# Linear attention in a decoder step: the norm factor of the prompt's chunks taken ahead of the decoded tokens and by tables, the gate applied to four chunks at a time

## The chip, the cores and the metric

One core of a Trainium2 chip. The metric is the time of one execution on the device, in microseconds, lower is better. Its engines here: TensorE (PE), VectorE (DVE), ScalarE (ACT), GpSimd (POOL) and SyncE (SP), whose queue issues most of the DMAs. TensorE's granted clock is 0.996 of its full 2.4 GHz in the profiled execution.

## The reference, cut to what matters

One layer of a hybrid decoder: 1024 prompt tokens and 8 sequences of 8 decoded tokens, width 1024. The part in question is the gated linear attention: 4 heads, key width 128, value width 256. Its output is normalised per token and head, multiplied by a gate, and projected:

```python
o_b, gla_state = gla_fn(q_b, k_b, v_b, log_alpha)
o_b = rmsnorm(o_b, g_gla).reshape(b, t, B_VAL_WIDTH) * jax.nn.silu(r_b)
merged = jax.nn.sigmoid(gate_a) * (o_a @ w_proj_a) + jax.nn.sigmoid(gate_b) * (o_b @ w_proj_b)
# rmsnorm: xf * lax.rsqrt(jnp.mean(xf * xf, axis=-1, keepdims=True) + EPS)
```

## The kernel before

A token axis of 1088 (1024 prompt, 64 decoded) lies along the free axis or, in tiles of 128, on the partitions. Heads h = 0 to 3 of the linear attention run one after the other, from about 655 us to 1060 us of the span. For each head:

- *Levels*: the decayed scores inside a chunk of 128 tokens are built by halving, levels 64, 32, 16, 8, 4, 2, 1 and 0. For each level with a decay, DVE subtracts twice into a tile with the tag `wv` (five buffers; also used for other tiles of its size), ACT takes the exponential (L1128), DVE multiplies half of it by q and POOL the other half by k (L128 is the helper of all tensor_tensor operations), and PE multiplies the blocks (`S<-wv`). Then `ke`, another `wv` tile: a subtraction over 1024 and one over 64 columns, an exponential (L1182) and a product with k.
- `v` comes from the input projection as `vT` (copied out of PSUM by ACT, L630, in three pieces), is transposed by PE (`tp<-idt,vT`) and split into `vh` and `vl`.
- *Gate*: sil[0], sil[1] = silu of r times the norm's gain, both with features on the partitions; sil[0] in a `wv` tile, sil[1] in a `vT` tile (in head 3 one with the name `bc`).
- *Chunks* 0 to 7: products `o`, copied to `ob` (L1251), squares summed into columns 0 to 7 of `gss`, and the state update.
- *Samples* r = 0, 1: four decoded sequences each; outputs `obs`, squares in columns 8 and 9 of `gss`, new states `so` stored (L1297).
- *Norm and gate*: rsqrt_mean makes the factor of all ten columns on DVE (a first guess by integer arithmetic and three steps); normed (L1304) scales one 128x256 tile; PE transposes it in two halves (L125); DVE multiplies each half by the gate into `oo` (two buffers), which SP stores to d_ob as 128x2x128 (L1321) or, for the samples, 128x2x32 (L1329).

PE has more to do than these: products of the input projection's next column groups (heads 0 to 2; `mm`) or of the first output projection, project_a (head 3), are laid between the steps as filler. A call of slot() emits a number of them in proportion to the list SLOTS_CHUNKS (sum 31). From the first chunk to the last gate product the order of PE's products is recorded and kept. Everything else is put in order on each engine by a scheduler, and pool buffers decide what must wait. After head 3 d_ob is loaded again (L1379, eight slices of 128x1088), split into `bh` and `bl`, and multiplied with w_proj_b, whose weights come in as `wraw` (L273), split by ACT (`whi`) and DVE (`wlo`).

The table form of the factor, rsqrt_mean_tables, is used elsewhere in the kernel: the mean on DVE, Ln and Exp on ACT, one step on DVE.

Of the kernel before, what the change touches and what calls it, by code (L numbers as in the profile page):

```python
# [11 lines left out]
ALU = mybir.AluOpType  # L12
# [4 lines left out]
P = 128  # L17
D = 1024
KD = D // P
T = 1024  # L20
NB, NS = 8, 8
TS = NB * NS
TT = T + TS
HA, DA = 8, 64
HB, DKB, DVB = 4, 128, 256
# [60 lines left out]
SLOTS_FOX = [c for n in range(15) for c in ((n + 1) % 8 + 3, n % 2 == 0, n % 8 + 3)]  # L86
SLOTS_DEC = [2] * 5 + [2, 2, 1, 1, 1, 2, 2, 2, 2] * 7 + [4] * 4
SLOTS_LEVELS = [4] * 8 + [2, 2]
SLOTS_CHUNKS = [1] + [2] * 10 + [1] * 10


@with_exitstack
def hybrid_step(ctx, tc, I, O):
# [8 lines left out]
    def new(pl, shape, tag, dt=F32, bufs=None):  # L102
        kw = {} if bufs is None else {"bufs": bufs}
        return pl.tile(shape, dt, tag=tag, name=nm(tag), **kw)
# [19 lines left out]
    def tr(*args):  # L124
        return record(pe.transpose(*args))  # L125

    def tt(eng, out, a, b, op):
        eng.tensor_tensor(out=out, in0=a, in1=b, op=op)  # L128
# [25 lines left out]
    ident = idt[:, :]  # L154
# [91 lines left out]
    def rsqrt_mean_tables(pl, ss, n, dim, cols=1):  # L246

        v = new(pl, [P, cols], "rs_v")
        dve.tensor_scalar(v[:n], ss, 1.0 / dim, EPS, ALU.mult, ALU.add)
        r = rsqrt_guess(pl, v[:n], n, cols)  # L250
        rsqrt_step(pl, v[:n], r, n, cols)
        return r
# [630 lines left out]
    with mkpool(name="dec", bufs=2, side="right") as dec:  # L883
# [98 lines left out]
        slot = spread(SLOTS_DEC)  # L982
# [65 lines left out]
    with mkpool(name="gla", bufs=1, side="right") as gp:  # L1048
# [9 lines left out]
        for h in range(HB):  # L1058
# [208 lines left out]
                slot()  # L1267
            sp.dma_start(out=O["gla_p"][0, 0, h], in_=st)


            obs = new(gp, [P, 2, DVB], "obs")
            for r in range(2):
                po = new(ps_o, [P, 256], "o")
                sts = []
                for x in range(4):
                    b = 4 * r + x
                    sb = new(gp, [P, DVB], "sb", bufs=4)
                    sp.dma_start(out=sb, in_=I["state_gla"][0, b, h])
                    sts.append(sb)
                for x in range(4):  # L1280
                    b = 4 * r + x
                    mm(po[32 * x:32 * x + 32, :], lhsT=qes[:, b, :], rhs=sts[x], start=True, stop=False)
                for x in range(4):
                    b = 4 * r + x
                    mm(po[32 * x:32 * x + 32, :], lhsT=axs[:, b, :], rhs=vns, start=False, stop=True)
                act.activation(obs[:, r, :], po, AF.Copy)
                jk = new(gp, [P, DVB], "jk", mybir.dt.bfloat16)
                act.activation(jk, obs[:, r, :], AF.Square, accum_out=ss[:, 8 + r:9 + r])
                for x in range(4):
                    b = 4 * r + x  # L1290
                    km = new(gp, [96, P], "km", F32R, bufs=2)
                    pool.tensor_scalar(km, f(k3[r]), cst[:96, K_MX - K_LV + x:K_MX - K_LV + x + 1], None, ALU.mult)
                    pst = new(ps_a, [P, 512], "S")
                    mm(pst[:, :DVB], lhsT=km, rhs=v3[r], start=True, stop=True)
                    so = new(gp, [P, DVB], "so", bufs=2)
                    stt(so, sts[x], eb[:, 8 + b:9 + b], pst[:, :DVB], ALU.mult, ALU.add)
                    sp.dma_start(out=O["gla_s"][0, b, h], in_=so)  # L1297
                slot()


            rs = rsqrt_mean(gp, ss, P, DVB, cols=10)
            def normed(i):
                src = ob[:, i, :] if i < 8 else obs[:, i - 8, :]
                dve.tensor_scalar(src, src, rs[:, i:i + 1], None, ALU.mult)  # L1304
                return src

            na = 3
            srcs = [normed(i) for i in range(na)]
            for i in range(10):
                if i + na < 10:  # L1310
                    srcs.append(normed(i + na))
                slot()
                src = srcs[i]
                tp = new(ps_a, [P, 512], "tp")
                for v in range(2):
                    tr(tp[:, v * P:(v + 1) * P], src[:, v * P:(v + 1) * P], ident)
                if i < 8:
                    oo = new(gp, [P, 2, P], "oo", bufs=2)
                    for v in range(2):
                        tt(dve, oo[:, v, :], tp[:, v * P:(v + 1) * P], sil[v][:, i * P:(i + 1) * P], ALU.mult)  # L1320
                    sp.dma_start(out=d_ob[2 * h:2 * h + 2, :, i * P:(i + 1) * P].rearrange("v p t -> p v t"), in_=oo)  # L1321
                else:
                    o = T + 32 * (i - 8)
                    oo = new(gp, [P, 2, P], "oo", bufs=2)
                    for v in range(2):
                        tt(dve, oo[:, v, :32].rearrange("p (b t) -> p b t", t=NS),
                           tp[:, v * P:(v + 1) * P].rearrange("p (b t) -> p b t", t=32)[:, :, :NS],
                           sil[v][:, o:o + 32].rearrange("p (b t) -> p b t", t=NS), ALU.mult)
                    sp.dma_start(out=d_ob[2 * h:2 * h + 2, :, o:o + 32].rearrange("v p t -> p v t"), in_=oo[:, :, :32])  # L1329
            pinned[0] = False  # L1330
            if h < HB - 1:
                drain()
# [723 lines left out]
```

## Time and profile before

| | us |
|---|---|
| median of 3 runs | 2026.95 (2025.34 to 2031.42) |
| the profiled execution | 2028.32 |
| its span in the profile | 2026.6 |
| PE busy in it | 1953.4 |
| DVE busy | 1315.1 |
| ACT busy | 910.8 |
| POOL busy | 461.5 |

The profile page gives the busy time of every engine, and the trace behind it each instruction with its start, its length and, where its engine had been idle, how long and what ended that idle time. PE is the busiest engine throughout, so the views to read are its idle time and what ended it.

### The profile page before, as it was taken

To read this page: it belongs to the slowest core of one execution; us is meant where nothing else is said; L and a number is where in the kernel's file an instruction comes from. 1 tells how busy PE (TensorE), PEld (TensorE's weight loads), DVE (VectorE), ACT (ScalarE), POOL (GpSimd) and SP (SyncE) were. 2 spreads that over 40 slices of the span, in tenths; PEclk is the share of its full clock that TensorE was granted. 3 is DMA by queue.
4 is the path that set the end of the run, shared out by engine and by line. 5 is a ranking of instruction groups with operands and counts; after the bars stand their busy time and mean duration, and the time that the engine had idled before them with its cause. 6 is when DMAs were issued, how large, how long until landed. Compare 5 with 4: busy or idle time off the path is not lost.

```text
span 2026.6 us, 35542 instructions
## 1 busy us (share of the span) xinstructions
PE 1953.4 (96%) x13681; PEld 1789.9 (88%) x13681; DVE 1315.1 (65%) x2635; ACT 910.8 (45%) x1734; POOL 461.5 (23%) x610
## 2 busy tenths in 40 slices
PE   6999999999999899999999999999999999999998
PEld 5899999997888788888989977899999999977886
DVE  6566665663334786868464457877677677758686
ACT  5344544442333465564544333454444444545552
POOL 2032323232110432313012221123223334210000
PEclk9999999999999999999999999999999999999999
DMA  4387979797883152423387442143444555657575
GB/s 139 96 200 182 230 184 204 172 223 269 284 267 110 43 136 60 120 60 99 105 263 233 151 156 104 41 143 129 145 132 144 195 181 171 224 194 244 175 251 158
DMA packets 302431, 335.25 MB, mean 165 GB/s; under 512 B 23327, under 2 KB 234575, under 8 KB 298165
## 3 DMA queue, kind: packets, MB, share of 16 engines
q1 hardware_dynamic: 216501, 217.37, 34.9%
q0 software_dynamic: 39488, 79.15, 15.4%
q10 hardware_dynamic: 46272, 36.44, 5.7%
q8 instruction: 108, 1.77, 0.4%
q14 instruction: 62, 0.51, 0.1%
HBM read 265.78 MB, written 113.30 MB: 187 GB/s over the span
## 4 chain that ended last, share of the span: by engine, by line
PE 77%; DVE 9%; DMA 6%; ACT 4%; issue 2%; POOL 1%; ACTq 1%; DVEq 0%; SPq 0%; POOLq 0%
PE mm L122 37%; PE dn L122 15%; PE u L122 9%; PE tp L125 5%; PE o L122 4%; PE S L122 3%; PE y L122 3%; DVE wv L128 2%; DMA d_ob<-oo 2%; DVE wlo L128 1%; DMA smk<-in_consts 1%; ACTq L195 1%; PE sm L122 1%; DMA m<-d_ob 1%; DVE act L128 1%
## 5 line engine op out<-in xcount | busy, mean ns | idle before, releaser
L122 PE MATMUL mm<-act,whi 128*128 128x384 f32 (+2 forms) x3568 | 891.1, 331 | 5.5 <-DVE act L128 3.9
L122 PEld LDWEIGHTS mm<-act,whi 128*128 128x128 f32 (+1 forms) x3568 | 617.1, 189 | 15.6 <-DVE act L128 5.4
L122 PE MATMUL mm<-act,wlo 128*128 128x384 f32 (+2 forms) x1784 | 583.2, 327 | 0.0
L122 PEld LDWEIGHTS mm<-act,wlo 128*128 128x128 f32 (+1 forms) x1784 | 336.3, 189 | 0.5
L128 DVE TENSOR_TENSOR wlo<-wraw,whi 128x1024 fp32r<-128x1024 f32 (+1 forms) x111 | 135.1, 1217 | 57.3 <-ACT whi L134 53.9
L134 ACT ACTIVATE whi<-wraw 128x1024 fp32r<-128x1024 f32 (+1 forms) x113 | 115.9, 1025 | 87.2 <-PE mm L122 79.1
L131 DVE SCALAR_TENSOR_TENSOR cv<-u,cw,cv 128x1104 f32<-128x1104 f32 x84 | 112.8, 1363 | 13.0 <-ACT cv L1556 13.0
L122 PE MATMUL dn<-dh,hhi 128*128 128x512 f32 x264 | 105.0, 400 | 2.4 <-ACT hhi L134 2.4
L122 PE MATMUL dn<-dh,hlo 128*128 128x512 f32 x264 | 104.8, 397 | 0.3 <-DVE hlo L128 0.3
L122 PE MATMUL dn<-dl,hhi 128*128 128x512 f32 x264 | 105.0, 398 | 0.0
L122 PE MATMUL y<-wo,act 128*128 128x512 f32 x416 | 99.8, 397 | 1.3 <-DVE wo L128 1.1
L122 PEld LDWEIGHTS y<-wo,act 128*128 128x128 f32 x416 | 77.1, 188 | 21.2 <-DVE wo L128 2.2
L134 ACT ACTIVATE sh<-sr 128x512 fp32r<-128x512 f32 x80 | 50.3, 633 | 87.1 <-PE u L122 33.3
L722 POOL TENSOR_SCALAR_AFFINE_SELECT bd<-cb 128x128 f32<-128x128 f32 x64 | 36.8, 582 | 179.8 <-DVE mx L739 163.3
L745 ACT ACTIVATE s<-s,ng 128x128 f32<-128x128 f32 (+3 forms) x64 | 49.6, 775 | 48.8 <-DVE ng L743 46.5
L420 ACT ACTIVATE spl<-mm 128x384 f32<-128x384 f32 (+1 forms) x72 | 33.6, 468 | 84.4 <-PE mm L122 74.4
L128 POOL TENSOR_TENSOR wv<-wv,k 128x512 f32<-128x512 f32 (+1 forms) x28 | 51.8, 1868 | 73.2 <-ACT wv L1128 72.1
L122 PE MATMUL mm<-bh,whi 128*128 128x384 f32 (+1 forms) x192 | 63.0, 328 | 3.2 <-ACT bh L134 2.6
L134 ACT ACTIVATE pth<-tp 128x512 fp32r<-128x512 f32 (+2 forms) x96 | 43.5, 488 | 49.3 <-PE tp L125 16.9
L735 DVE CUSTOM_DVE_ANT_0 s<-S,cb 128x512 f32<-128x512 f32 (+2 forms) x80 | 40.7, 527 | 37.9 <-PE S L122 32.4
L1556 ACT ACTIVATE cv<-u,cw 128x1104 f32<-128x1104 f32 x42 | 54.9, 1308 | 22.0 <-issue 10.8
L200 POOL DMA_DIRECT2D d_ws<-in_w_up x40 | 53.9, 1542 | 41.1 <-DMA d_ws<-in_w_up 40.7
(470 smaller groups left out, 4281.5 us busy)
## 6 DMA issues: line engine op xcount, KB each, us to landing
wraw<-in_w_in SPq DMA_DIRECT2D x52, 512.0 KB
wraw<-in_w_up SPq DMA_DIRECT2D x44, 512.0 KB
d_ws<-in_w_up ACTq DMA_DIRECT2D x80, 256.0 KB
sr<-d_ws SPq DMA_DIRECT2D x80, 256.0 KB
draw<-in_w_down SPq DMA_DIRECT2D x77, 256.0 KB
d_h<-cv POOLq DMA_DIRECT2D x44, 256.0 KB, 5.0
d_s<-spl POOLq DMA_DIRECT2D x44, 256.0 KB, 4.8
d_ws<-in_w_up POOLq DMA_DIRECT2D x40, 256.0 KB, 9.2
```

The costliest lines, as they stand in the source:

```text
L122: return record(pe.matmul(out, **kw))
L125: return record(pe.transpose(*args))
L128: eng.tensor_tensor(out=out, in0=a, in1=b, op=op)
L131: return dve.scalar_tensor_tensor(out=out, in0=a, scalar=s, in1=b, op0=op0, op1=op1)
L134: act.activation(out, src, AF.Copy)
L195: act.dma_start(out=d, in_=y)
L200: pool.dma_start(out=d_ws[i][d], in_=src, max_dma_last_dim=4 * P * 4, accum_op=ALU.add)
L420: act.activation(t[:, o:o + n], ps[:, :n], AF.Copy)
L722: pace[1] = pool.affine_select(out=bd, in_=cb[:, qc], pattern=[[-1, P]], compare_op=ALU.is_ge, fill=NEG, base=0, channel_multiplier=1)
L735: dve.tensor_tensor_reduce(out=s[:, k0:k0 + m], in0=ps[:, :m], in1=cb[:, k0:k0 + m], scale=1.0, scalar=-3.0e38, op0=ALU.add, op1=ALU.max, ...
L745: pace[0] = act.activation(s[:, :nk], s[:, :nk], AF.Exp, bias=ng, accum_out=sm)
L1556: act.activation(c, u[:, 2:], AF.Identity, scale=cw[:, 2, m:m + 1], bias=cw[:, 3, m:m + 1])
```

## The change

The factor of the eight prompt columns is taken right after the chunks by rsqrt_mean_tables, ahead of the samples; the eight `ob` tiles are normalised four at a time behind the samples' state updates (L1271). After the samples the factor of the two sample columns follows, again by tables. The result tile `oo` becomes two tiles of 128x1088, one per half of the values, with the tag `wv`. In four steps PE transposes four chunks into one PSUM bank, DVE multiplies 128x512 and SP stores 128x512 (L1320); a fifth step does the samples. SLOTS_CHUNKS has 16 entries where it had 21, with the same sum. The table form is:

```python
v = new(pl, [P, cols], "rs_v")
dve.tensor_scalar(v[:n], ss, 1.0 / dim, EPS, ALU.mult, ALU.add)
act.activation(r[:n], v, AF.Ln)
act.activation(r[:n], r[:n], AF.Exp, scale=-0.5)
# then on DVE: q = r*r*v; q = 1.5 - 0.5*q; r = r*q
```

```diff
--- before.py
+++ after.py
@@ -86,7 +86,7 @@
 SLOTS_FOX = [c for n in range(15) for c in ((n + 1) % 8 + 3, n % 2 == 0, n % 8 + 3)]
 SLOTS_DEC = [2] * 5 + [2, 2, 1, 1, 1, 2, 2, 2, 2] * 7 + [4] * 4
 SLOTS_LEVELS = [4] * 8 + [2, 2]
-SLOTS_CHUNKS = [1] + [2] * 10 + [1] * 10
+SLOTS_CHUNKS = [1] + [2] * 15
 
 
 @with_exitstack
@@ -1267,6 +1267,11 @@
                 slot()
             sp.dma_start(out=O["gla_p"][0, 0, h], in_=st)
 
+            def normed(src, r):
+                dve.tensor_scalar(src, src, r, None, ALU.mult)
+
+            rs = rsqrt_mean_tables(gp, ss[:, :8], P, DVB, cols=8)
+
 
             obs = new(gp, [P, 2, DVB], "obs")
             for r in range(2):
@@ -1295,38 +1300,34 @@
                     so = new(gp, [P, DVB], "so", bufs=2)
                     stt(so, sts[x], eb[:, 8 + b:9 + b], pst[:, :DVB], ALU.mult, ALU.add)
                     sp.dma_start(out=O["gla_s"][0, b, h], in_=so)
+                for i in range(4 * r, 4 * r + 4):
+                    normed(ob[:, i, :], rs[:, i:i + 1])
                 slot()
 
 
-            rs = rsqrt_mean(gp, ss, P, DVB, cols=10)
-            def normed(i):
-                src = ob[:, i, :] if i < 8 else obs[:, i - 8, :]
-                dve.tensor_scalar(src, src, rs[:, i:i + 1], None, ALU.mult)
-                return src
-
-            na = 3
-            srcs = [normed(i) for i in range(na)]
-            for i in range(10):
-                if i + na < 10:
-                    srcs.append(normed(i + na))
-                slot()
-                src = srcs[i]
-                tp = new(ps_a, [P, 512], "tp")
+            rs = rsqrt_mean_tables(gp, ss[:, 8:], P, DVB, cols=2)
+            for r in range(2):
+                normed(obs[:, r, :], rs[:, r:r + 1])
+            oo = [new(gp, [P, TT], "wv", bufs=5) for _ in range(2)]
+            for half in range(2):
+                c = slice(512 * half, 512 * half + 512)
                 for v in range(2):
-                    tr(tp[:, v * P:(v + 1) * P], src[:, v * P:(v + 1) * P], ident)
-                if i < 8:
-                    oo = new(gp, [P, 2, P], "oo", bufs=2)
-                    for v in range(2):
-                        tt(dve, oo[:, v, :], tp[:, v * P:(v + 1) * P], sil[v][:, i * P:(i + 1) * P], ALU.mult)
-                    sp.dma_start(out=d_ob[2 * h:2 * h + 2, :, i * P:(i + 1) * P].rearrange("v p t -> p v t"), in_=oo)
-                else:
-                    o = T + 32 * (i - 8)
-                    oo = new(gp, [P, 2, P], "oo", bufs=2)
-                    for v in range(2):
-                        tt(dve, oo[:, v, :32].rearrange("p (b t) -> p b t", t=NS),
-                           tp[:, v * P:(v + 1) * P].rearrange("p (b t) -> p b t", t=32)[:, :, :NS],
-                           sil[v][:, o:o + 32].rearrange("p (b t) -> p b t", t=NS), ALU.mult)
-                    sp.dma_start(out=d_ob[2 * h:2 * h + 2, :, o:o + 32].rearrange("v p t -> p v t"), in_=oo[:, :, :32])
+                    slot()
+                    tp = new(ps_a, [P, 512], "tp")
+                    for i in range(4):
+                        tr(tp[:, i * P:(i + 1) * P], ob[:, 4 * half + i, v * P:(v + 1) * P], ident)
+                    tt(dve, oo[v][:, c], tp, sil[v][:, c], ALU.mult)
+                    sp.dma_start(out=d_ob[2 * h + v, :, c], in_=oo[v][:, c])
+            slot()
+            tp = new(ps_a, [P, 512], "tp")
+            for v in range(2):
+                for r in range(2):
+                    tr(tp[:, (2 * v + r) * P:(2 * v + r + 1) * P], obs[:, r, v * P:(v + 1) * P], ident)
+            for v in range(2):
+                tt(dve, oo[v][:, T:].rearrange("p (b t) -> p b t", t=NS),
+                   tp[:, 2 * v * P:2 * (v + 1) * P].rearrange("p (b t) -> p b t", t=32)[:, :, :NS],
+                   sil[v][:, T:].rearrange("p (b t) -> p b t", t=NS), ALU.mult)
+                sp.dma_start(out=d_ob[2 * h + v, :, T:], in_=oo[v][:, T:])
             pinned[0] = False
             if h < HB - 1:
                 drain()
```

Where the instructions stand now: on DVE in head 0, before, from the second half of the samples to the norm's first operation. `wv<-bc` are subtractions of the next head's levels, `wv<-wv,q` their multiplies, `so` the samples' new states, `rs_v` the mean of the norm.

```order
L131 SCALAR_TENSOR_TENSOR so_8518<-sb_8480,eb_8079,S_8516 128x256
L128 TENSOR_TENSOR wv_8829<-wv_8829,q_8157 128x16x32
L128 TENSOR_TENSOR wv_8882<-bc_8120 128x32x16
L128 TENSOR_TENSOR wv_8941<-bc_8120 128x64x8 x2
L131 SCALAR_TENSOR_TENSOR so_8565<-sb_8542,eb_8079,S_8563 128x256
L131 SCALAR_TENSOR_TENSOR so_8572<-sb_8544,eb_8079,S_8570 128x256
L128 TENSOR_TENSOR wv_8882<-wv_8882,q_8157 128x32x16
L128 TENSOR_TENSOR wlo_8812<-wraw_8809,whi_8811 128x1024
L128 TENSOR_TENSOR wv_8941<-wv_8941,q_8157 128x64x8
L131 SCALAR_TENSOR_TENSOR so_8579<-sb_8546,eb_8079,S_8577 128x256
L131 SCALAR_TENSOR_TENSOR so_8586<-sb_8548,eb_8079,S_8584 128x256
L213 TENSOR_SCALAR rs_v_8602<-gss_8166 128x10
```

Twelve of the level operations of the next head (levels 64 to 8) stand here or just ahead, among the samples. After, on DVE at the same place, from the samples' last new state on; `wv<-tp` are now the gate multiplies.

```order
L131 SCALAR_TENSOR_TENSOR so_8600<-sb_8562,eb_8079,S_8598 128x256
L128 TENSOR_TENSOR wv_8633<-tp_8675,vT_8299 128x512
L128 TENSOR_TENSOR wv_8766<-bc_8120 128x8x64 x2
L128 TENSOR_TENSOR wv_8803<-bc_8120 128x16x32 x2
L128 TENSOR_TENSOR wv_8632<-tp_8694,wv_8217 128x512
L128 TENSOR_TENSOR wv_8766<-wv_8766,q_8157 128x8x64
L128 TENSOR_TENSOR wv_8803<-wv_8803,q_8157 128x16x32
L128 TENSOR_TENSOR wv_8633<-tp_8715,vT_8299 128x512
L128 TENSOR_TENSOR wv_8632<-tp_8742,wv_8217 128x64
L128 TENSOR_TENSOR wv_8633<-tp_8742,vT_8299 128x64
L128 TENSOR_TENSOR wv_8856<-bc_8120 128x32x16
L128 TENSOR_TENSOR wlo_8846<-wraw_8843,whi_8845 128x1024
```

Those twelve operations now stand between and behind the gate multiplies. On SP in head 3, before, from the last stores of the gate on (`m<-d_ob` and `sg<-d_ob` load d_ob again, `d_m<-act` stores a column group of project_a, `wraw<-in_w_proj_b` loads weights):

```order
L1329 DMA d_ob_67<-oo_12618 128x2x32
L1039 DMA d_m_10_71<-act_2114_11797 128x1088
L273 DMA wraw_12886<-in_w_proj_b 128x8x128
L1379 DMA m_2283_12664<-d_ob_67 128x1088
L1379 DMA m_2284_12672<-d_ob_67 128x1088
L1379 DMA sg_12680<-d_ob_67 128x1088
L1039 DMA d_m_10_71<-act_2114_11797 128x1088
L1379 DMA m_2286_12688<-d_ob_67 128x1088
```

The first weights are issued ahead of all of these loads of d_ob. After, on SP at the same place:

```order
L1330 DMA d_ob_67<-wv_12347 128x64
L1032 DMA act_2086_11721<-d_ga_68 128x1088
L1039 DMA d_m_10_71<-act_2084_11719 128x1088
L1380 DMA m_2243_12560<-d_ob_67 128x1088
L1380 DMA m_2244_12568<-d_ob_67 128x1088
L1380 DMA sg_12576<-d_ob_67 128x1088
L1039 DMA d_m_10_71<-act_2084_11719 128x1088
L1380 DMA m_2246_12584<-d_ob_67 128x1088
L1380 DMA m_2247_12592<-d_ob_67 128x1088
L1039 DMA d_m_10_71<-act_2086_11721 128x1088
L273 DMA wraw_12782<-in_w_proj_b 128x8x128
L1380 DMA m_2248_12600<-d_ob_67 128x1088
```

The loads of d_ob moved ahead of the first weights of w_proj_b, which now follow a later store of project_a. On ACT in head 3, after, around the sample columns' factor (L231 is the Ln, L232 the Exp, L1034 project_a's sigmoid; before, one table load stands in the whole of head 3):

```order
L231 ACT_TABLE_LOAD
L231 ACTIVATE rs_r_12336<-rs_v_12334 128x2
L1034 ACT_TABLE_LOAD
L1034 ACTIVATE act_2086_11721<-act_2086_11721 128x1088
L232 ACT_TABLE_LOAD
L232 ACTIVATE rs_r_12336<-rs_r_12336 128x2
L134 ACTIVATE whi_12395<-wraw_12393 128x512
L1034 ACT_TABLE_LOAD
L1034 ACTIVATE act_2084_11719<-act_2084_11719 128x1088
```

Each change of function between these three now has a load of its table.

## Rows read from the trace of the kernel before

**Rows 1.** The page, part 1: busy us, share of the span, instructions of each engine.

```profile
PE 1953.4 (96%) x13681; PEld 1789.9 (88%) x13681; DVE 1315.1 (65%) x2635; ACT 910.8 (45%) x1734; POOL 461.5 (23%) x610
```

**Rows 2.** List of waits of PE, 690 to 1090 us: us in total, times, longest.

```profile
PE tp L125 <- DVE ob L1304: 3.9, 3, 1.3
PE mm L122 <- ACT bh L134: 2.6, 1, 2.6
PE tp L125 <- DVE vl L128: 2.3, 3, 0.8
...
PE S L122 <- DVE so L131: 1.9, 1, 1.9
PE tp L125 <- ACT vT L630: 1.9, 3, 1.0
```

**Rows 3.** Timeline of PE, head 0 to 1: start us, us, instruction, [idle before <-releaser].

```profile
742.00 0.39 PE L122 MATMUL S<-v,km 96*128 96x256 f32 x1
...
748.58 0.70 PE L125 MATMUL tp<-idt,ob 128*128 128x128 f32 x4 [1.33 <-DVE ob L1304]
...
776.25 0.44 PE L125 MATMUL tp<-idt,vT 128*128 128x128 f32 x2 [0.96 <-ACT vT L630]
```

**Rows 4.** Timeline of DVE in the same stretch, columns as above.

```profile
744.51 0.48 DVE L213 TENSOR_SCALAR rs_v<-gss 128x10 f32<-128x10 f32 x1
...
748.17 1.14 DVE L1304 TENSOR_SCALAR ob<-ob,rs_r 128x256 f32<-128x256 f32 x4
...
764.26 0.19 DVE L128 TENSOR_TENSOR oo<-tp,wv 128x32 f32<-128x32 f32 x1 [1.88 <-DMA d_ob<-oo]
...
768.23 2.15 DVE L128 TENSOR_TENSOR wv<-wv,q 128x544 f32<-128x544 f32 x1
...
773.51 0.21 DVE L128 TENSOR_TENSOR wv<-bc 128x64 f32<-128x64 f32 x1
```

**Rows 5.** Timeline of POOL in the same stretch.

```profile
739.25 6.94 POOL L128 TENSOR_TENSOR wv<-wv,k 128x512 f32<-128x512 f32 x4 [0.36 <-ACT k L630]
...
767.88 3.99 POOL L128 TENSOR_TENSOR wv<-wv,k 128x544 f32<-128x544 f32 x2 [3.81 <-ACT wv L1128]
```

**Rows 6.** Timeline of ACT in the same stretch.

```profile
773.81 1.11 ACT L1182 ACTIVATE wv<-wv 128x1088 f32<-128x1088 f32 x1 [3.97 <-DVE wv L128]
...
775.78 0.42 ACT L630 ACTIVATE vT<-mm 128x320 f32<-128x320 f32 x1
```

**Rows 7.** List of waits of all engines, 690 to 1090 us.

```profile
DVE oo L128 <- DMA d_ob<-oo: 12.0, 15, 1.9
```

**Rows 8.** Instructions by tile or line: count, ns min/median/max, first and last start, forms.

```profile
L128 DVE TENSOR_TENSOR oo<-tp,wv x40: 178/284/294, 749.2 to 1058.0; 128x128 f32<-128x128 f32 x32, 128x32 f32<-128x32 f32 x8
...
L128 DVE TENSOR_TENSOR wv<-bc x64: 209/696/2652, 658.1 to 959.3; 128x512 f32<-128x512 f32 x32, 128x544 f32<-128x544 f32 x24, 128x1024 f32<-128x1024 f32 x4, 128x64 f32<-128x64 f32 x4
...
L128 DVE TENSOR_TENSOR act<-tp,act x36: 415/683/693, 10.3 to 1306.7; 128x512 fp32r<-128x512 f32 x32, 128x256 fp32r<-128x256 f32 x4
```

**Rows 9.** Timeline of SP's queue in head 3.

```profile
1059.39 0.39 SPq L273 DMA_DIRECT2D wraw<-in_w_proj_b  x1
...
1069.92 0.38 SPq L1039 DMA_DIRECT2D d_m<-act  x1
...
1075.58 0.32 SPq L1379 DMA_DIRECT2D m<-d_ob  x1
```

**Rows 10.** Timeline of PE at the end of head 3.

```profile
1073.31 0.33 PE L122 MATMUL mm<-bh,whi 128*128 128x384 f32 x1
...
1082.59 0.44 PE L122 MATMUL mm<-bh,whi 128*128 128x384 f32 x1 [2.65 <-ACT bh L134]
```

**Rows 11.** Timeline of ACT in head 3.

```profile
1018.72 1.28 ACT L1034 ACT_TABLE_LOAD   x1 [1.57 <-DMA act<-d_ga]
1020.02 1.11 ACT L1034 ACTIVATE act<-act 128x1088 f32<-128x1088 f32 x1
...
1033.02 0.63 ACT L134 ACTIVATE whi<-wraw 128x512 fp32r<-128x512 f32 x1 [5.71 <-PE mm L122]
```

## Prediction

> **What bounds the kernel now.** I read the page first: TensorE (PE) is busy 96% of the span [rows 1], so only the few microseconds in which it stands still can be won. Then the list of waits of PE over the attention stretch, 690 to 1090 us [rows 2]. Five waits matter: 3.9 us in three times for the normalised `ob`, 1.9 for `vT`, 2.3 for `vl`, 1.9 once for `so`, 2.6 once for `bh`. The first three come once in each of heads 0 to 2. The PE timeline of head 0 shows the pair [rows 3]: 1.33 us ahead of the first transposes at 748.58, then 0.96 us at 776.25 for the last piece of `vT`. The second wait is the important one. Its cause stands in the ACT rows [rows 6]: `vT` is copied at 775.78, right behind an exponential that ACT began at 773.81 after idling 3.97 us for VectorE (DVE); DVE's last subtraction ahead of it ends at 773.7 [rows 4]. So in each head a DVE chain, from the samples' last state update through norm, gate multiplies and the next head's level operations to that subtraction, sets when PE goes on. Time won at the norm is kept only if this chain ends earlier too; otherwise PE waits just as much longer at 776.
>
> **The change part by part, heads 0 to 2.** I count what DVE does on that chain, before and now, against an end of 773.7.
>
> Removed. The ten-column factor runs from 744.51 to 748.17 [rows 4], 3.7 us; two columns by tables keep a mean, four small operations of the kind in those rows and two on ACT, some 0.9: -2.8. Eight of ten normalisations go between the samples; four take 1.14 us [rows 4], 0.285 each: -2.3 here. They fall where DVE waits for PE, so I cost them at nothing there; if that cover were gone they would cost their 2.3. The gate: sixteen multiplies of 0.284 and four of 0.18 [rows 8] are 5.3 us laid end to end, about 4.3 with neighbours overlapping as the normalisations do; four of 128x512 with a PSUM operand (0.683, the `act<-tp` row of [rows 8]) and two small ones make 3.1: -1.2. The waits of the gate multiplies for the stores that free `oo`, 12.0 us over four heads [rows 7], an example 1.88 at 764.26 [rows 4]: -3.0 a head, since both new tiles hold a whole head. And the chain begins earlier: the twelve level operations that stood among the samples are gone from there, so the last state update can follow PE's last sample product (742.00, [rows 3]) by 0.4 where rs_v now starts at 744.51, 2.5 after it: -2.1. Sum: -11.4.
>
> Added. The two new tiles come from the same five buffers as the level tiles, and the order shows the effect: those twelve operations (levels 64 to 8, 128x512) now stand between and behind the gate multiplies. At 0.68 with slight overlap, 0.65 each (median 0.696 over all forms, [rows 8]): +7.8. GpSimd's four multiplies of these levels move with them; they took 6.94 us together among the samples [rows 5], 1.74 each, and DVE slows beside them: the multiply at 768.23 takes 2.15 us [rows 4] for a form whose median is some 0.7, next to 3.99 us of two GpSimd multiplies [rows 5]. That is 0.7 to 1.4 us a GpSimd multiply: +2.8 to +5.6. The other idle of the chain (waits on ACT and PE) I leave as it is: the gate multiplies now wait for quads of transposes that the order puts 12 to 18 projection products apart, which takes the place of like waits.
>
> Net: -0.8 to +2.0 a head; I take +0.6, the middle, since some operations beside GpSimd read PSUM and the first two quads overlap with little. So `vT` is ready at 776 to 778, PE having reached it 1.3 us earlier: the 1.33 us at the norm go, the wait at 776.25 grows by 1.3 to 2. For three heads: -2.4 to +6.0, taken +1.8. That transposes come in fours saves PE little, as it waits behind them anyway.
>
> How GpSimd and DVE share is where the page speaks: the Trainium skill, "SBUF — State Buffer", section "Who interferes with whom", says that a DVE instruction with two SBUF inputs and a GpSimd instruction that reads SBUF exclude each other for a whole instruction. This trace agrees in part: the 768.23 multiply lost about 1.4 us beside 3.99 us of GpSimd. By the page's rule the four moved multiplies would block up to 4 x 1.74 = 7.0 us of DVE instead of 5.6, and the sum per head could reach +3.4.
>
> **Head 3.** No next head follows, so the gate chain only has slack to lose: PE's waits here are 1.9 for `so` (its place in the order is unchanged, kept) and 2.65 at 1082.59 for `bh` [rows 10]. The latter is a late load of a slice of d_ob: issued at 1075.58 [rows 9], its first product at 1082.59, 7.0 us with the split. On SyncE's queue the loads of d_ob now stand ahead of the first weights of the second projection, which were issued at 1059.39 [rows 9] and now come behind the store that goes out at 1069.92 [rows 9]. The d_ob loads thus start some 4 us sooner and the 2.65 us go. But the weights, 512 KB against the 557 KB of that slice, are issued at 1070.3 and by the same 7.0 us come to their first product at 1077.3, while PE wants them at 1073.31 [rows 10]: 4.0 us lost, 3.0 if the load is 1 us quicker as the queue ahead of it has thinned, and up to 5.3 with the wait for their low part, which DVE makes behind ACT (1.3 at most, since ACT's own part of the split is already in the 7.0). Net of the 2.65 won: +0.4 to +2.7; I take +1.2, and -0.5 as the low end in case the store goes out a little sooner.
>
> The tables cost loads in this head, since the sigmoids of the projection lie between: the order has seven loads where one stood. One takes 1.28 us [rows 11]; six more are 7.7 us on ACT, which idles 5.71 us in one piece here, up to 1033.02 [rows 11]. I cost them at nothing, for idle of that kind hides them; if it did not, DVE's projection evacuations, which stand behind the factor in its order, would be late by as much. The Trainium skill, "ScalarE: Activation LUTs", section "What ACT_TABLE_LOAD costs", gives 1.28 us and a drain of 1.38 beside it. The trace agrees with the first figure and shows the next activation at 1020.02, right behind the load [rows 11]; with a drain each time six would be an estimated 16 us, no longer hidden entirely.
>
> Sum: 2028.32 (the profiled execution) +1.8 +1.2 = 2031.3. The median of the runs, 2026.95, is 1.4 below that execution; I predict against the median: 2026.95 + 3.0, rounded to 2030.0.
>
> **Rivals.** What this kernel's timing can tell from no change is about 0.3%, 6.1 us: 2020.9 and 2033.0.
> 1. *The gain stays* (faster). DVE hides more than I think: GpSimd costs nothing and the chain ends 2 us sooner or more. Then the norm's 3.9 go, up to 1.9 + 2.3 of the later waits with them, and head 3 brings up to 2.7. The whole is -10.8, 2016.2; the middle between that and the norm's 3.9 alone, -7.4, gives 2019.6. For: 3 us of store waits a head vanish for certain. Against: the moved work, 7.8 us, outweighs them. 0.15.
> 2. *The chain gets longer* (slower): level operations behind the gate run against GpSimd and the end of the subtraction slips past 775.5 in heads 0 to 2. At +2.0 to +3 a head and +2.3 in head 3: +8.3 to +11, 2036. It decides for slower from (6.1 - 1.2) / 3 = 1.6 us a head. For: the 2.15 us multiply. Against: the earlier start by 2.1. 0.24.
> 3. *Table loads surface in head 3*: DVE waits in order for the factor, with the projection's evacuations and state updates behind it, and PE for those. At most 7.7 us, likelier 3: about 2033, on the border. 0.06.
> 4. *The change does not do what it says* in the sense that the factor ahead of the samples holds up the state updates instead: eight normalisations, 2.3 us, delay each head's samples; +2.3 x 3, with the rest as forecast about 2037. 0.05, since PE's last sample product sets that end.
>
> My own case, no change that can be told, 2024 to 2033, has 0.50; rival 3 lies half on either side of the border.
>
> **How the numbers follow.** Faster: rival 1, 0.15. Slower: 0.24 and 0.05 and half of 0.06, 0.32. Same: 0.50 and the other half, 0.53. The range: from 2020.5, which leaves out half of rival 1, to 2036.5, which leaves out the worst of rivals 2 and 4.
>
> **What would show it.** In the changed profile: no wait of DVE for stores to d_ob at the gate; no wait of PE for `ob`; larger waits of PE for `vT` (2 to 3 us in place of 0.6 to 1.0, three times); the subtraction ahead of that exponential ending within 2 us of 773.7; GpSimd's multiplies after 748; in head 3 a wait of 3 to 5 us of PE for the weights at 1073 and none at 1082; seven table loads with no wait of PE behind them. The prediction is wrong if the `vT` waits stay below 1 us (rival 1), or grow beyond 3.5 us (rival 2).

## The result, and the profile after

| | before | after |
|---|---|---|
| median, us | 2027.18 (2025.34 to 2031.42, 5 runs) | 2044.51 (2033.31 to 2047.16, 5 runs) |
| profiled execution | 2028.32 | 2033.31 |
| its span | 2026.6 | 2031.5 |
| mean granted clock of the runs after | | 0.994, 0.987, 0.988, 0.989, 0.992 |

The ratio after to before is 1.0063, with a 95% interval of 1.0033 to 1.0092: slower. (The quotient of the medians is larger, 1.0085: of the five runs after, the fastest lies 7 us under the next. The trace shown below is of that fastest run.) Forecast was 2030.0, between 2020.5 and 2036.5; the median lies outside. The direction that I held second most likely came, by a cause that is in none of the rivals.

PE's list of waits after, 690 to 1100 us (engine, line, waited for: us in total, times, longest):

```profile
PE tp L125 <- ACT vT L630: 13.0, 3, 4.3
PE o L122 <- ACT ob L1251: 1.9, 3, 0.7
PE mm L122 <- ACT whi L134: 1.9, 1, 1.9
PE S L122 <- DVE so L131: 1.6, 1, 1.6
```

Against [rows 2] the 3.9 us for `ob`, the 2.3 for `vl` and the 2.6 for `bh` are gone, and `vT` has gone from 1.9 to 13.0 us, 4.3 in each of three heads. The wait that the change removed comes back at the second place, three times as long. The timelines of head 0 say why: PE, then DVE, ACT and POOL.

```profile
739.55 0.29 PE L122 MATMUL S<-v,km 96*128 96x256 f32 x1
...
774.35 0.44 PE L125 MATMUL tp<-idt,vT 128*128 128x128 f32 x2 [4.33 <-ACT vT L630]
```

```profile
744.55 2.49 DVE L128 TENSOR_TENSOR wv<-bc 128x512 f32<-128x512 f32 x4
746.95 0.68 DVE L128 TENSOR_TENSOR wv<-tp,wv 128x512 f32<-128x512 f32 x1
747.55 3.06 DVE L128 TENSOR_TENSOR wv<-wv,q 128x512 f32<-128x512 f32 x2
...
769.60 2.09 DVE L128 TENSOR_TENSOR wv<-wv,q 128x544 f32<-128x544 f32 x1
771.61 0.21 DVE L128 TENSOR_TENSOR wv<-bc 128x64 f32<-128x64 f32 x1
```

```profile
771.91 1.11 ACT L1182 ACTIVATE wv<-wv 128x1088 f32<-128x1088 f32 x1 [4.20 <-DVE wv L128]
...
773.88 0.42 ACT L630 ACTIVATE vT<-mm 128x320 f32<-128x320 f32 x1
```

```profile
747.07 2.99 POOL L128 TENSOR_TENSOR wv<-wv,k 128x512 f32<-128x512 f32 x2 [11.80 <-ACT wv L1128]
...
766.41 4.69 POOL L128 TENSOR_TENSOR wv<-wv,k 128x544 f32<-128x544 f32 x2 [3.54 <-ACT wv L1128]
```

The whole trace of after is 2.45 us ahead at the last sample product (739.55 against 742.00, [rows 3]): ahead of that place the granted clock of before fell (0.66 in 670 to 675 us, 0.87 and 0.79 in 685 to 695), that of after did not. So I count from the sample product. The chain up to the end of the subtraction that starts at 771.61 takes 32.3 us (31.7 before, [rows 4]); from the sample product to PE's transposes of the last `vT` piece it is 34.80 us against 34.25. The level operations stand where the order said, and DVE's two multiplies at 747.55 take 3.06 us beside POOL's 2.99.

So the wait is 3.4 us longer, but PE goes on only 0.55 us later. Yet from the last sample product of one head to that of the next, after takes 96.14 us (head 0 to 1) and 96.19 (1 to 2) where before takes 93.22 and 92.88: 2.9 and 3.3 us more. Most of the rest shows in another column. PE's busy time and granted clock in 5 us stretches of after (stretch, length, PE busy, clock, DMA share, GB/s):

```profile
770.00:775.00 5.00, 0.67 (x5) 1.00 0.00 0
775.00:780.00 5.00, 5.00 (x84) 0.66 0.42 108
...
870.00:875.00 5.00, 4.53 (x81) 0.66 0.41 108
...
965.00:970.00 5.00, 3.34 (x74) 0.62 0.18 54
970.00:975.00 5.00, 5.00 (x70) 0.69 0.01 4
```

Behind each of the three waits TensorE runs for some microseconds at its lower level (1.2 GHz, half of 2.4): (1 - 0.66) x 5 = 1.7 us lost in heads 0 and 1, 3.4 in head 2. In the trace of before the clock is 1.00 in all of the corresponding stretches:

```profile
765.00:795.00 30.00, 28.27 (x509) 1.00 0.09 22
860.00:890.00 30.00, 28.77 (x488) 1.00 0.15 38
955.00:990.00 35.00, 33.35 (x517) 1.00 0.16 49
```

### The profile page after: what moved, and what is told of

It is laid out like the page before. It is cut to its first block, busy times and chain, and to the rows that moved or that the text cites. A ratio compares the mean times of both kernels' runs of the same rounds, so it can differ in the third digit from the quotient of the medians.

```text
span 2031.5 us, 35451 instructions
## 1 busy us (share of the span) xinstructions
PE 1955.2 (96%) x13681; PEld 1792.4 (88%) x13681; DVE 1313.4 (65%) x2571; ACT 923.4 (45%) x1757; POOL 461.6 (23%) x610
## 4 chain that ended last, share of the span: by engine, by line
PE 80%; DVE 8%; ACT 4%; DMA 4%; issue 2%; POOL 1%; ACTq 1%; SPq 0%; DVEq 0%; POOLq 0%
PE mm L122 40%; PE dn L122 15%; PE u L122 9%; PE tp L125 5%; PE o L122 5%; PE S L122 4%; PE y L122 3%; DVE wv L128 2%; PE sm L122 1%; DMA smk<-in_consts 1%; ACTq L195 1%; ACT whi L134 0%; DMA hraw<-d_hs 0%; DVE rs_q L131 0%; DVE wlo L128 0%
## 5 line engine op out<-in xcount | busy, mean ns | idle before, releaser
L1557 ACT ACTIVATE cv<-u,cw 128x1104 f32<-128x1104 f32 x42 | 54.9, 1309 | 21.5 <-DVE u L131 10.1
L122 PEld LDWEIGHTS dn<-dh,hhi 128*128 128x128 f32 x264 | 49.7, 188 | 15.5 <-ACT hhi L134 4.3
```

The lines of the kernel that those rows point to most:

```text
L122: return record(pe.matmul(out, **kw))
L1557: act.activation(c, u[:, 2:], AF.Identity, scale=cw[:, 2, m:m + 1], bias=cw[:, 3, m:m + 1])
```

## The experiments

Each kernel ran beside the kernel before, whose medians were 2029.8 (first four), 2032.1 (next four) and 2030.8 (last three). The table gathers what follows; "waits" are PE's for `vT` and `vl` in the three heads, "lost there" is (1 - clock) times the length of the stretches 765:795, 860:890 and 955:990 together, in one trace each.

| kernel | median | ratio to before, 95% | waits, us | lost there, us |
|---|---|---|---|---|
| before | 2027.2 | | 1.9 + 2.3 | 0 |
| after | 2044.5 | 1.0063 (1.0033 to 1.0092) | 13.0 | 7.1 |
| e1_again | 2040.3 | 1.0045 (1.0030 to 1.0061) | 13.0 | 6.9 |
| e2_busy_pe | 2047.3 | 1.0081 (1.0058 to 1.0104) | 3.6 + 4.1 | 3.6 |
| e3_copy_first | 2037.4 | 1.0028 (1.0011 to 1.0045) | 8.1 | 10.1 |
| e4_in_place | 2025.9 | 0.9975 (0.9957 to 0.9992) | 0.5 | 0 |
| e5_in_place_weights | 2017.5 | 0.9931 (0.9916 to 0.9947) | 0.4 | 0 |
| e6_pairs_wv | 2050.6 | 1.0103 (1.0085 to 1.0121) | 13.9 | 8.6 |
| e7_early_factor | 2025.8 | 0.9972 (0.9957 to 0.9986) | 0 | 0 |
| e8_factor_on_dve | 2043.2 | 1.0047 (1.0028 to 1.0065) | 13.1 | 5.4 |
| e9_quads_late_factor | 2029.4 | 0.9988 (0.9975 to 1.0001) | 0.5 | 0 |
| e10_early_factor_weights | 2026.6 | 0.9975 (0.9963 to 0.9987) | 0 | 0 |
| e11_weights_only | 2041.3 | 1.0036 (1.0020 to 1.0051) | 13.2 | 6.9 |

**e1_again.** The same program.

> The changed kernel once more, for a second trace and more times. Theory (clock): each of heads 0 to 2 ends its level chain late, PE waits about 4.3 us for the copy of vT, and after each such wait TensorE's granted clock falls to its lower level for some microseconds, longer in some executions than in others. Expected 2033 to 2047 us with mean clocks of 0.987 to 0.994; the rows with a clock below 0.9 follow the vT waits, and the time not explained by the clock stays near 2028. Rival (fixed cost): the loss lies in waits alone; then the waits of PE would differ from those of the first trace by as much as the times do.

Median 2040.3 of 11 runs, 2033.8 to 2044.9, clocks 0.989 to 0.993. The waits are those of the first trace to 0.1 us for `vT`, and the time of this execution is 2041.19 against 2033.31. The clock differs (same columns as above):

```profile
480.00:485.00 5.00, 5.00 (x18) 0.50 0.48 138
...
780.00:785.00 5.00, 3.49 (x75) 0.50 0.24 65
...
880.00:885.00 5.00, 5.00 (x90) 0.83 0.39 105
...
975.00:980.00 5.00, 5.00 (x87) 0.77 0.19 56
```

The three falls are there again, with another depth each, and there are falls elsewhere (480 us) in work that the change does not touch. At the three places the two traces lose about the same, 7.1 and 6.9 us; the 7.9 us between their times lie with falls elsewhere, above all 3.4 us at 470 to 490 us and 3.4 at 670 to 700, where the first trace has none. Taken over the runs: span times (1 - mean clock) has a median of 20.4 us here and of 12.2 us in the 28 runs of before beside it, 8.2 of the 10.5 us between the medians; what is left of the times once it is taken away is 2020.8 against 2019.5. That sum is rough, since the mean clock has three digits (2 us) and work at half clock can hide other waits (e2), but it puts most of the loss on the clock. No run holds the clock up with the wait left as it is: that share is read from the clock column, not from an experiment of its own.

**e2_busy_pe.** After, with products that nobody reads in the place of the wait:

```diff
-                        tr(ps[:n, i, :], st_v["vT"][:, o:o + n], ident)
+                        if h and half == 0 and i0 == 4 and i == 2:
+                            for _ in range(32):
+                                ins = mm(ps[:, 2:4, :], lhsT=hn_h[0][:, 0, :P], rhs=hn_h[0][:, 0, :2 * P],
+                                         start=True, stop=True)
...
+                        last_, last = (last if i else None), tr(ps[:n, i, :], st_v["vT"][:, o:o + n], ident)
...
```

The lines left out keep these products between the two transposes in PE's order.

> The changed kernel with 32 products of 128x256 that nobody reads put on PE ahead of the transposes that wait for the last piece of vT, in heads 1 to 3's levels: some 3.8 of the 4.3 us of the wait are then filled, and all else is left. Theory (clock): the granted clock no longer falls there, so 5 to 7 us less than the profiled execution of the changed kernel, 2024 to 2030, mean clock at least 0.996, and a spread like that of the kernel before. Rival (the chain alone costs): the chain ends when it did, so the time stays 2033 to 2047 or rises by what the products overlap, up to 1 us a head.

2047.3 us: the theory's 2024 to 2030 failed. PE's waits and the fall behind the first of the three places (lines are shifted by 5 in this kernel):

```profile
PE tp L125 <- DVE vl L133: 5.4, 4, 1.4
PE tp L125 <- ACT vT L635: 3.6, 3, 1.2
PE mm L122 <- ACT whi L139: 3.6, 1, 3.6
```

```profile
785.00:790.00 5.00, 5.00 (x86) 0.73 0.25 74
```

Each group of products takes 4.08 us, and the clock still falls at two places of three, behind waits of 1.2 and 1.4 us that follow the products. The loss there halves (3.6 for 7.1), but waits for `vl`, which after does not have at these places, come back (4.1 more), the wait for the weights grows by 1.7 (by 0.6 against e1), and the three groups cost 12.2 us where 9.4 us of waiting went: +8.6 together, against 3.5 us less lost to the clock. Giving PE something to do instead of nothing is no cure here; and which work keeps the clock up, these runs do not settle.

**e3_copy_first.** After, with ACT's exponential behind the copy of the last piece of `vT` (the list `copies`, in lines left out, holds the three copies):

```diff
...
-            act.activation(ke, ke, AF.Exp, scale=1.0 / 16)
+            with tc.issue_after(copies[2].ins):
+                act.activation(ke, ke, AF.Exp, scale=1.0 / 16)
```

> The changed kernel with the exponential of ke put behind the copy of the last piece of vT on ACT, so that this copy no longer waits for DVE's level chain. Theory: the vT waits of 4.3 us fall to under 1 us, no clock falls, 2020 to 2027 us: the 4 us won at the norm in heads 0 to 2 are kept in part, with vl and the last level's product as the next late things. Rival (the chain is needed anyway): PE waits as long a little later, for the level products or for ke's use in the chunks, and the time stays above 2033.

2037.4 us: the wait moved, as the rival said.

```profile
PE tp L125 <- DVE vl L128: 9.4, 4, 2.7
```

```profile
975.00:980.00 5.00, 5.00 (x21) 0.50 0.16 46
```

`vT` no longer waits, but `vl` stands in DVE's order behind the same chain; behind 2.7 us in each head the clock falls at all three places, for longer than in after.

**e4_in_place.** After, with the gate's result written into the gate's own tiles, which frees the two `wv` buffers:

```diff
-            oo = [new(gp, [P, TT], "wv", bufs=5) for _ in range(2)]
+            oo = sil
```

> The changed kernel with the gate multiplied in place (the result goes into the gate's own tiles), so that no two further buffers are taken from the level tiles. Theory: the next head's level operations stand among the samples again, DVE's chain ends some 3 us earlier, the vT waits fall to 0 to 2 us, 2020 to 2028 us. Rival (buffers don't matter, the tables or the quads of transposes are what is late): vT waits stay at 4 us and the time above 2033.

2025.9 us, faster than before by 0.25%. In the order the next head's level operations stand among the samples again. The chain is shorter than in before: from the last sample product to the transposes of the last `vT` piece it takes 31.0 us in each of heads 0 to 2 (before 34.3, 33.7 and 34.0, after 34.8). There is no wait for `vT` and no fall at the three places. The late weights of head 3 are now the longest wait:

```profile
PE mm L122 <- ACT whi L134: 5.9, 1, 5.9
```

**e5_in_place_weights.** The same, with the first weights of the second projection ahead of the loads of d_ob:

```diff
+        units(8)
+        first_w = load_split(wpool, w["w_proj_b"][:, :P], KD, P)
...
```

`units(8)` lays up to eight of the remaining groups of filler products ahead of that load; it is part of this edit, here and in e10 and e11.

> The in-place kernel, and the first weights of the second projection asked for ahead of the loads of d_ob in head 3, as in the kernel before. Theory: the wait of PE for those weights (5.9 us in the in-place kernel) and the fall of the clock behind it (3.2 us) go: 2016 to 2021 us, faster than both kernels by 0.3 to 0.6%. Rival (the loads of d_ob become late instead, as in the kernel before, where PE waited 2.6 us for them): 2021 to 2025.

2017.5 us (2014.2 to 2022.6), 0.69% faster than before and the best of all, with a mean clock of 0.995. The weights' wait is gone, no new one stands in its place, and the one for `bh` is 0.3 us:

```profile
PE S L122 <- POOL wv L128: 5.6, 3, 2.8
PE o L122 <- ACT ob L1251: 2.0, 3, 0.7
PE S L122 <- DVE so L131: 1.9, 1, 1.9
```

The first of these belongs to head 0's own levels, ahead of the change's work.

**e6_pairs_wv.** Before, with one thing of the change alone: two full-length `wv` tiles for the gate's result, stored 128x512 at a time.

```diff
+            both = [new(gp, [P, TT], "wv", bufs=5) for _ in range(2)]
...
-                        tt(dve, oo[:, v, :], tp[:, v * P:(v + 1) * P], sil[v][:, i * P:(i + 1) * P], ALU.mult)
+                        tt(dve, both[v][:, i * P:(i + 1) * P], tp[:, v * P:(v + 1) * P], sil[v][:, i * P:(i + 1) * P], ALU.mult)
...
```

> The kernel before with one thing of the change alone: the gate's result goes into two full-length tiles from the level tiles' five buffers, stored 128x512 at a time; factor and pairs of transposes as before. Theory (buffers): the next head's level operations move behind the gate as in the changed kernel, PE waits 3 to 5 us for vT in each of three heads on top of the 1.3 us for ob, and clocks fall behind it: 2040 us or more. Rival (the early factor or the quads are what delays the chain): no such wait, 2024 to 2032.

2050.6 us: the buffers alone do the harm. The chain takes 36.6 us in each of heads 0 to 2. (The larger stores are part of this edit too, but e4 and e9 have them without harm.)

```profile
PE tp L125 <- ACT vT L630: 13.9, 3, 4.8
```

The expected wait for `ob` on top did not come.

**e7_early_factor.** Before, with the factor alone changed (eight columns by tables ahead of the samples, two behind); gate, pairs and small `oo` buffers as before.

```diff
...
+            rs = rsqrt_mean_tables(gp, ss[:, :8], P, DVB, cols=8)
+
             obs = new(gp, [P, 2, DVB], "obs")
...
-            rs = rsqrt_mean(gp, ss, P, DVB, cols=10)
...
+            rs = rsqrt_mean_tables(gp, ss[:, 8:], P, DVB, cols=2)
...
```

> The kernel before with the factor alone changed: eight columns ahead of the samples and two behind, both by tables; the gate in pairs through the two small oo buffers as before. Theory: the waits for ob (3.9 us in three times) go, the level operations stay among the samples, the chain ends 0 to 3 us earlier since the stores still hold oo up: 2022 to 2030. Rival (tables): the seven table loads in head 3 delay the projection's evacuations, PE waits 3 us or more between 1020 and 1060: above 2031.

2025.8 us, 0.28% faster than before. The waits for `ob` and `vT` are gone; the weights of head 3 are late (3.8 us), and at the norm there is left

```profile
PE tp L125 <- DVE oo L128: 3.5, 4, 1.9
```

**e8_factor_on_dve.** After, with rsqrt_mean in the place of rsqrt_mean_tables at both places.

```diff
-            rs = rsqrt_mean_tables(gp, ss[:, :8], P, DVB, cols=8)
+            rs = rsqrt_mean(gp, ss[:, :8], P, DVB, cols=8)
...
-            rs = rsqrt_mean_tables(gp, ss[:, 8:], P, DVB, cols=2)
+            rs = rsqrt_mean(gp, ss[:, 8:], P, DVB, cols=2)
```

> The changed kernel with its two factors computed on DVE by the integer guess and three steps in place of the tables, at the same places. Theory: the chain behind the samples grows by some 2.5 us on DVE, the vT waits go from 4.3 to 4 to 7 us, nothing is won in head 3: 2038 to 2050. Rival (table loads cost the time): without the six loads the time falls by 3 us or more, below 2037.

2043.2 us, 1.0047: no faster than after (e1: 1.0045). The table loads of head 3 cost nothing that can be told, and the factor's way of being computed is not what counts: the `vT` waits are 13.1 in place of 13.0 us.

**e9_quads_late_factor.** In place as in e4, but with the factor of all ten columns behind the samples on DVE: the quads and the larger stores alone.

```diff
...
-            rs = rsqrt_mean_tables(gp, ss[:, 8:], P, DVB, cols=2)
+            rs = rsqrt_mean(gp, ss, P, DVB, cols=10)
+            for i in range(8):
+                normed(ob[:, i, :], rs[:, i:i + 1])
...
```

> The in-place kernel with the factor where and how the kernel before has it (ten columns behind the samples, on DVE): quads and larger stores alone. Theory (the early factor is worth the wait for ob, the quads the waits for the oo stores): PE waits 1.3 us or more for ob in heads 0 to 2 again, the chain is no later than in the kernel before, weights of the second projection late as in the in-place kernel: 2026 to 2032, 2 to 5 us above the in-place kernel. Rival (the quads win everything): as the in-place kernel, 2023 to 2026.

2029.4 us, 0.9988 (0.9975 to 1.0001): not told from before. PE's waits from 655 to 1100 us:

```profile
PE mm L122 <- ACT whi L134: 6.5, 1, 6.5
...
PE tp L125 <- DVE ob L1271: 4.0, 3, 1.3
```

The waits for `ob` are back as expected, and the weights of head 3 are late.

**e10_early_factor_weights.** e7 with e5's early weights.

> The kernel before with the early factor by tables (gate in pairs, small oo buffers) and the first weights of the second projection ahead of the loads of d_ob. Theory (weights late cost 4 us of waiting and 3 us of clock): 2018 to 2022. Rival (the pairs' waits for oo stores keep the gain away): 2022 to 2027.

2026.6 us, no better than e7. The 3.8 us that e7 waited for the weights became

```profile
PE mm L122 <- DVE act L128: 4.5, 1, 4.5
```

at the same product. What is late now is the last gate tile of project_a: its load goes out at 1062.59 on SP (in e5 the last one goes out at 1043.15), ACT's sigmoid of it begins at 1069.34 after waiting for that load, and only behind it can DVE take project_a's last three results out of PSUM:

```profile
1070.48 1.42 DVE L128 TENSOR_TENSOR act<-mm,act 128x384 f32<-128x384 f32 x3 [2.21 <-ACT act L1034]
```

```profile
1071.09 0.44 PE L122 MATMUL mm<-bh,whi 128*128 128x384 f32 x1 [4.49 <-DVE act L128]
```

So in the pairs' form the early weights win nothing.

**e11_weights_only.** After with e5's early weights.

> The changed kernel with the first weights of the second projection ahead of the loads of d_ob, and nothing else. Theory: head 3's wait of 2 to 3 us for the weights goes and the vT waits of 4.3 us with their falls of the clock stay: 2035 to 2040, still slower than the kernel before. Rival (head 3 is what costs the time): 2030 or less.

2041.3 us, 1.0036: still slower than before. Head 3 is not where the time went.

## Why the prediction was wrong

*What bounds the kernel, and that a gain at the norm returns at `vT`*: right. The waits for `ob` went and those for `vT` grew. e4 and e7, where the chain ends earlier, keep the gain.

*The chain in heads 0 to 2, +0.6 us a head*: right in its sum (its parts were not measured one by one). From the last sample product to the transposes of the last piece of `vT` the three heads take 0.55, 1.06 and 0.83 us more than before: 2.4, forecast 1.8. DVE slowed beside POOL as priced: two multiplies of some 0.7 us took 3.06 beside 2.99 us of POOL, 0.8 us for each of POOL's, inside the 0.7 to 1.4 that I took.

*The wait at 776, "grows by 1.3 to 2"*: mis-sized. It went from 0.96 to 4.33 us, by 3.4, and past the 3.5 us that I had named as a sign of being wrong. (In before the three `vT` waits are 0.96, 0.45 and 0.44 us, not 0.6 to 1.0 as I wrote.) PE reached it 2.8 us earlier, not 1.3: of that 1.33 is the wait for `ob`, and 0.8 the transposes, ten groups of 0.38 us before and five of 0.60 now, which I had put at little; 0.7 I have not placed. By itself this would not have cost anything, as the chain sets the end.

*What I did not price, and the step that failed*: I took a longer wait to cost its length and nothing more, with TensorE at full clock behind it. The granted clock is 1.00 at these places in the trace of before, and I did not ask what it does when PE stands for 4 us there. At these places the traces agree: at all three it fell in each of the six traces whose waits there are 2.7 us or longer (after, e1, e3, e6, e8, e11), and at none in the six whose waits are at most 1.0 us (before, e4, e5, e7, e9, e10); e2, between, has it at two of three. Each fall costs 1.7 to 3.5 us, 5.4 to 10.1 us for the three. In the terms of my sum: the chain came to 2.4 us for the 1.8, head 3's late load to -0.8 in the trace of after (1.86 us of waiting for 2.65) for the +1.2, and the clock, which has no term in it, to 7.1 in after and 6.9 in e1.

Elsewhere the length of a wait does not settle whether the clock falls. The wait of 2.65 us for `bh` in before [rows 10] has no fall behind it (1.00 from 1080 to 1090 us), one of 1.92 us at 670.16 has (0.66); and in after

```profile
684.58 0.80 PE L122 MATMUL S<-wv 128*32 128x32 f32 x68 [2.78 <-POOL wv L128]
```

```profile
685.00:690.00 5.00, 5.00 (x130) 1.00 0.29 87
690.00:695.00 5.00, 5.00 (x36) 1.00 0.00 0
```

where nearly the same wait in before, 2.74 us at 687.27, has 0.87 and 0.79. What else decides it stays open.

The Trainium skill, "TensorE: Matmul & The Clock Gate", section "Part 1: The HAM clock gate (the "warmup" mystery)", says that the throttled clock is the state of rest and that activity releases it; the traces agree in that the clock fell behind PE's standing still at these places and came back while PE worked (0.66 in 775:780 of after, 1.00 in 780:785); the 0.50 of a stretch such as 480:485 in e1 is the lower level. That page was open to me, and I did not ask what its rule would make of a change which gathers PE's idle time into one piece. Here such a piece was paid for twice, with its length and with the clock behind it.

*Head 3*: the order did put the weights late, and the load took what I gave it: issued at 1072.81, first product at 1079.58, 6.8 us (forecast 7.0). PE waited 1.9 us (3.0 in e1), not 4.0, since it came there later itself. The wait of 2.65 us for `bh` [rows 10] is gone. SP and PE of after:

```profile
1072.81 0.43 SPq L273 DMA_DIRECT2D wraw<-in_w_proj_b  x1
```

```profile
1079.58 0.44 PE L122 MATMUL mm<-bh,whi 128*128 128x384 f32 x1 [1.86 <-ACT whi L134]
```

*Rival 3, table loads*: refuted by e8, and by the trace of after, where PE's only waits between 1000 and 1090 us are 1.56 for `so` and 1.86 for the weights. The loads are one more than I counted: eight stand in head 3 of after where one stood, so seven more, 9.0 us on ACT in place of 7.7. They stand in ACT's idle time as the order said, two of them here:

```profile
1040.28 1.28 ACT L231 ACT_TABLE_LOAD   x1
1041.57 0.20 ACT L231 ACTIVATE rs_r<-rs_v 128x2 f32<-128x2 f32 x1
1041.80 1.28 ACT L1034 ACT_TABLE_LOAD   x1
```

The next activation begins 0.01 us behind each of these loads. The drain of 1.38 us that the Trainium skill gives in "ScalarE: Activation LUTs", section "What ACT_TABLE_LOAD costs", and that I quoted, does not show.

*Rival 4, the early factor delays the samples*: refuted by e7, which is faster than before.

*Rival 2, the chain gets longer*: its 2036 us is nearest to the time, but its mechanism was not the cause: the chain grew by 0.8 us a head, under the 1.6 from which it was to decide. Rival 1's mechanism is right where the buffers are left alone, as e4 and e5 show.

So the parts of the change are worth: the early factor by tables 0.28% faster (e7); quads and large stores without the two extra buffers no difference that can be told (e9), both together 0.25% (e4), and 0.69% with the weights in their old place in the queue (e5). The two `wv` tiles for the result turn that into 0.63% slower; alone, with the stores that go with them, they make the kernel before 1.03% slower (e6).

What stays open: what decides, beside a wait's length, whether the clock falls, why e10's last gate tile is loaded so late, the 0.7 us above, and some 0.6 us between each last piece of `vT` and the next head's samples beyond the clock's 1.7 (61.34 against 58.97 us in head 0, counted from `vT` to the last sample product).

## What to carry to other kernels

A tile taken from a pool that the next stage's work also uses moves that work: ask which operations stood ahead only because those buffers were free, and whether the result can go in place. A wait of PE is priced with its length and with what the granted clock does behind it: at the three places of this change one wait of 2.7 to 4.8 us had a fall behind it every time and waits of at most 1.0 us never, but two of 1.2 and 1.4 us close together (e2) had it at two places of three. When a change moves a load behind another on a queue, look at who needs it first.

## What the hardware showed that I had not expected

The time of one and the same program spreads with the clock: in 28 runs of the kernel before beside e1 it lay between 2024.6 and 2040.3 us, with mean clocks of 0.991 to 0.997. Falls occur in places that no edit touched (480, 670, 690, 1305, 1810 us), some in one trace and not in the next; a single profiled execution, such as the one at 2033.3 us here, can lie 11 us from the median of its kernel. And it may be that work at half clock hides another wait: before has 0.77 to 0.78 us of waiting for `vl` in each of the three heads and e2 1.35 to 1.36, while after, whose clock is low just there, has none. No run tests this.
